# One triangular-solve right-hand side computed as two accumulated products instead of one over stacked operands

## The chip, the cores and the metric

The kernel runs on one core of a Trainium2 chip. The time is the device time of one execution in microseconds (us); three executions are given before the change. The engines are named as in the profile: PE does matrix products, PEld is PE's weight load, DVE, ACT and POOL do element-wise work, SP issues transfers. Each engine works through its own queue of instructions in order and waits at an instruction for its semaphores.

## The reference, cut to what matters

The program is one layer of an encoder with three token mixers that run beside each other: an mLSTM, a long convolution, and a bidirectional RWKV-7 time mixing. The change touches the third alone. With 1024 positions, 16 heads of width 64 and two directions it computes for each head

```python
def step(state, inp):
    r_t, w_t, k_t, v_t, kk_t, a_t = inp
    sa = jnp.einsum('bhij,bhj->bhi', state, -kk_t)
    state = (state * w_t[:, :, None, :] + sa[..., None] * (kk_t * a_t)[:, :, None, :]
             + v_t[..., None] * k_t[:, :, None, :])
    return state, jnp.einsum('bhij,bhj->bhi', state, r_t)
```

once forwards and once backwards, and the outputs of the two directions are added. Everything is float32.

## The kernel before, in words

The projections of the input (`gemm`, L343 to L357) are long rows of matmuls of 128x512: each float32 operand is split into a high and a low part, and three products are summed, hence the lines L351, L352 and L353. Their weights come in by `load_w` (L327): a transfer `wraw`, a rounding to `wh` on ACT (L333), the remainder `wl` on POOL (L334). These projections are jobs in a list, and `fill` advances them by two 128-row pieces at a time.

The RWKV recurrence is computed in chunks of 64 positions. Two heads form a pair that fills 128 partitions (one head in 0 to 63, one in 64 to 127), and both directions go side by side, so eight pairs have 16 chunk steps each: 128 steps in all, in `scan` (L1733). `prep` makes the scaled vectors: `ar` holds alpha (`ar[:, 0]`, from the key directions) and the scaled receptance (`ar[:, 1]`), `bk` holds beta and the scaled keys. `tphase` makes the inverse triangular matrix `tt` of each chunk by a forward substitution on DVE (the many `tm` and `Tb` operations at L476). `setup` (L1659) makes for two chunks at a time the masked Gram matrices `G`, the transposes `B`, and the values in the lower half (partitions 64 to 127) of `SV`.

One step of `scan` is a chain:

- U: a right-hand side, in a bank of PSUM called `pch`. It has a values' part (masked Gram matrix times values) and a state's part (alpha times the state). Before the change both are one product over 128 rows: `G[0:64]` holds a copy of alpha, `SV[0:64]` a copy of the state. In the profile this is `pch<-SV,G`, four matmuls for two heads and two directions.
- `us` is U copied out of PSUM on DVE (L1762). `tt` times `us` gives SA (`pch<-us,tt`).
- SA is copied into `SV[0:64]`, over the state, one head by DVE (L1768), one by ACT (L1769).
- B times `SV` gives the change of the state (`pch<-SV,B`); two DVE operations at L476 add the old state and scale it, giving `sn`, the new state.
- `sn` is copied into the `SV[0:64]` of the next step, one head by DVE (L1793), one by ACT (L1794), and the next U starts.

The outputs of a step are put off into the next one (`late`): a product of `SV` and `G` (`pch<-G,SV`) stands right behind the next U, and a product of state and receptance (`pch<-ar,sn`) right behind the next SA.

What a matmul of float32 costs: the profile shows two records for each of these 64-wide matmuls, so a group of four appears as eight.

The order of an engine's queue is set when the program is built, by the framework's scheduler: it goes by its own estimate of when operands are ready, by priorities (`in_turn` gives the chain's matmuls the highest and keeps each group together in its given order), and by the order in which the code is written. `weave` spreads the projections' jobs evenly over the steps of the scan, so that each pair of chain products has projection matmuls between them on PE.

Of the kernel before, what the change touches and what calls it, by code (L numbers as in the profile page):

```python
# [285 lines left out]
class Trunk:  # L286
# [1060 lines left out]
    def rwkv(self, yc_out, pairs=range(8)):  # L1347
        nc, tc, A = self.nc, self.tc, self.A
        with ExitStack() as c2:
            e = c2.enter_context  # L1350
            cp = e(tc.tile_pool(name="rc", bufs=1))
            self.rp = e(tc.tile_pool(name="rp", bufs=1))
            self.oka = cp.tile([128, 8], F32, name="oka")
            nc.vector.tensor_scalar(self.oka, self.col("ka", 0, 8), -0.5, 1.0, op0=MUL, op1=ADD)


            self.hka = cp.tile([128, 8], F32, name="hka")
            nc.vector.tensor_scalar(self.hka, self.col("ka", 0, 8), 0.5, None, op0=MUL)
            self.hrk = cp.tile([128, 8], F32, name="hrk")
            nc.vector.tensor_scalar(self.hrk, self.col("rk", 0, 8), 0.25, None, op0=MUL)  # L1360
            self.nkk = cp.tile([128, 8], F32, name="nkk")
            nc.vector.tensor_scalar(self.nkk, self.col("kk", 0, 8), -0.5, None, op0=MUL)
            self.hwa = cp.tile([128, 32], F32, name="hwa")
            nc.vector.tensor_scalar(self.hwa, self.col("w0", 0, 32), 0.5, None, op0=MUL)
            self.hlgb = cp.tile([128, 16], F32, name="hlgb")
            nc.vector.tensor_scalar(self.hlgb, self.col("lg", 0, 16), 0.5, None, op0=MUL)
            self.gmask = cp.tile([128, 2, 128], F32, name="gmask")
            nc.sync.dma_start(self.gmask, A["gmask"])
            self.smask = cp.tile([128, 8 * 65], F32, name="smask")
            nc.vector.memset(self.smask, 1.0)  # L1370
            nc.vector.memset(self.smask.rearrange("p (c t) -> p c t", t=65)[:, :, 0:1], 0.0)
            self.bln = cp.tile([128, 1], F32, name="bln")
            nc.vector.memset(self.bln, 10.0 * math.log(2.0))


            self.tt_t = [p.tile([128, 16, CL], F32, name=f"tt{g}", tag=f"tt{g}", bufs=1)
                         for g, p in enumerate((self.ep, cp))]
            self.vp = self.ep.tile([128, T], F32, name="vp", tag="vp", bufs=1)

            self.cmat = cp.tile([128, 128], F32, name="cmat")  # L1380
            self.stt(self.cmat, self.ones_bd, -1.0 / 64.0, self.ident)
            for t in self.tt_t:
                nc.vector.memset(t, 0.0)


            pairs = list(pairs)
            n = len(pairs)
            cx = [dict(p=p, ar={}, al={}, bk={}, pc={}) for p in pairs]
            run(self.load(cx[0]))
            for g in range(2):  # L1390
                for d in range(2):
                    run(self.prep(cx[0], g, d))
                    self.fill(6)
                if g == 0:
                    for _ in self.tphase(cx[0], 0):
                        self.fill(1)
            prep1 = iter(())
            run(self.setup(cx[0], 0))
            for i in range(n):
                at = {}  # L1400

                def put(gen, *steps):
                    for s in steps:
                        at.setdefault(s, []).append(gen)
                put(prep1, 0, 0, 1, 2, 3, 4, 4)
                put(self.bonus(cx[i]), 5, 6, 7)
                put(ahead(tc, self.tphase(cx[i], 1), TP), *range(6, 28, 2))
                if i + 1 < n:
                    nx = cx[i + 1]
                    put(self.load(nx, cx[i - 1] if i else None), 8, 9, 10, 11)  # L1410
                    put(ahead(tc, self.prep(nx, 0, 0), PP), 15, 16, 19, 33, 33)
                    put(ahead(tc, self.prep(nx, 0, 1), PP), 34, 35, 36, 37, 37)
                    put(ahead(tc, self.tphase(nx, 0), TP), *range(39, 62, 2))
                    prep1 = ahead(tc, chain(self.prep(nx, 1, 0), self.prep(nx, 1, 1)), PP)
                    put(prep1, 40, 42, 49)
                if i > 0:
                    put(self.post(cx[i - 1], yc_out, i + 1 == n), 5, 6, 7, 8, 11, 12, 13, 14)
                weave(self.scan(cx[i], cx[i + 1] if i + 1 < n else None), at, self.fill, max(0, self.left() - 6) / (64.0 * (n - i + 0.1)))
            run(self.post(cx[n - 1]))
            return cx[n - 1]["out"]  # L1420
# [106 lines left out]
    def prep(self, cx, g, d):  # L1527

        nc, rp = self.nc, self.rp
        p, r, k, kk, w2, mm = (cx[n] for n in ("p", "r", "k", "kk", "w2", "mm"))  # L1530
# [43 lines left out]
        for q in range(2):  # L1574
            ar = self.ep.tile([128, 4, 2, CL], F32, name="ar", tag="ar", bufs=8)
            bk = self.ep.tile([128, 4, 2, CL], F32, name="bk", tag="bk", bufs=8)
            cs = slice(4 * q, 4 * q + 4)
            self.stt(ar[:, :, 0, :], c8(rd(kk))[:, cs], -2.0, P[:, cs, 0:64], MUL, MUL)
            self.tt(ar[:, :, 1, :], c8(rd(r))[:, cs], P[:, cs, 1:65])
            self.tt(bk[:, :, 0, :], c8(tmp)[:, cs], s[:, cs, 1:65])  # L1580

            self.tt(bk[:, :, 1, :] if d == 0 else bk[:, :, 1, ::-1], c8(a)[:, cs], s[:, cs, 1:65])
            for j in range(2):
                cx["al"][g, d, 2 * q + j] = ar[:, 2 * j:2 * j + 2, 0, :]
            for j in range(4):
                cx["ar"][g, d, 4 * q + j] = ar[:, j]
                cx["bk"][g, d, 4 * q + j] = bk[:, j]
            yield
# [70 lines left out]
    def setup(self, cx, b):  # L1659

        nc, rp, vp = self.nc, self.rp, self.vp
# [3 lines left out]
        g, c = b // 4, 2 * (b % 4)  # L1665
        hsl = (slice(0, 64), slice(64, 128))
        ops = [(j, d, cx["bk"][g, d, c + j], cx["ar"][g, d, c + j]) for j in range(2) for d in range(2)]

        G = rp.tile([128, 2, 2, 2, 128], F32, name="G", tag="G", bufs=2)
# [3 lines left out]
                     for j, d, bk, ar in ops for h in (1, 0))  # L1673
        for h in range(2):
            self.tt(G[:, :, :, h, :], pg[h], self.gmask.unsqueeze(1).broadcast_to([128, 2, 2, 128]))
            for d in range(2):
                nc.scalar.copy(G[0:64, :, d, h, 0:64], cx["al"][g, d, b % 4][hsl[h]])  # L1677
        yield


# [7 lines left out]
        if b < 4:  # L1688

            SV = rp.tile([128, 2, 4, 64], F32, name="SV", tag="SV", bufs=4)  # L1690
            if b == 0:
                nc.gpsimd.memset(SV[0:64], 0.0)
            cx["sv"].append(SV)
            pv = pv[:, 0:256].rearrange("p (e c) -> p e c", e=2)
            for e in range(2):
                t0 = 128 * (7 - b if e else b)
                nc.tensor.matmul(pv[:, e], vp[:, t0:t0 + 128], self.cmat, start=True, stop=True)
            for k in range(2):
                nc.scalar.copy(SV[64:128, :, 2 * k:2 * k + 2].rearrange("p h e x -> p e h x"),
                               pv[hsl[k]].rearrange("p e (h x) -> p e h x", h=2))  # L1700
            at = ((0, 3), (2, 1))
            SV = cx["sv"][b]
        else:
            SV = cx["sv"][7 - b]
            at = ((1, 2), (3, 0))
# [27 lines left out]
    def scan(self, cx, nx):  # L1733

        nc, rp = self.nc, self.rp
        S0 = None
        y = rp.tile([128, T], F32, name="y", tag="y", bufs=1)
        hsl = (slice(0, 64), slice(64, 128))
# [7 lines left out]
        now, late = chunk(0), None  # L1746
        for m in range(16):
            g, c, j = m // 8, m % 8, m % 2
            tt = self.tt_t[g]
            ar = [cx["ar"][g, d, c] for d in range(2)]  # L1750
            G, B, SV, at, both = now
            if j == 0:
                ahead = self.setup(cx, m // 2 + 1) if m < 14 else self.setup(nx, 0) if nx else iter(())
            ch = self.ps.tile([128, 4, 2, CL], F32, name="pch", tag="c", bufs=2)
            U, SA, SN, py = (ch[:, i] for i in range(4))

            ins = self.in_turn(partial(nc.tensor.matmul, U[hsl[h], d], G[:, j, d, h, 0:64], SV[:, h, at[d]],
                                       start=True, stop=True) for d in range(2) for h in (1, 0))
            if late:
                late[0](ins)  # L1760
            us = self.sm.tile([128, 2, CL], F32, name="us", tag="us", bufs=2)
            nc.vector.tensor_copy(us, U)  # L1762
            ins = self.in_turn(partial(nc.tensor.matmul, SA[hsl[h], d], tt[hsl[h], 8 * d + c, :], us[hsl[h], d],
                                       start=True, stop=True) for d in range(2) for h in range(2))
# [18 lines left out]
            S0 = S1  # L1783
# [3 lines left out]
            if m in (7, 15):  # L1787
                late[1](late[0](None))
                late = None
            if m < 15:  # L1790

                SV, at = now[2], now[4]
                nc.vector.tensor_copy(SV[0:64, 0, at], S1[0:64])  # L1793
                nc.scalar.copy(SV[0:64, 1, at], S1[64:128])  # L1794
            yield
            next(ahead, None)
            yield
# [111 lines left out]
```

## Time and profile before

| | us |
|---|---|
| median of three executions | 2141.99 |
| lowest and highest | 2134.19, 2142.42 |
| the profiled execution: its time | 2147.95 |
| the profiled execution: its span, first to last instruction | 2145.5 |
| stretch of the 128 chunk steps, first U to last output, from the span's start | 916 to 1933 |
| mean granted TensorE clock | 0.975 of full speed |

A row of the grouped view reads: line, engine, operation, written tile `<-` read tiles, shapes, `x` how many, then the time in which at least one of them ran, the mean duration of one in ns, and after the second bar the idle time of the engine just before them with what ended it. A row of the timeline reads: start, duration, engine, line, operation. Matmul records overlap, so the distance between two starts tells what one costs PE, not the duration of one.

### The profile page before, as it was taken

To read this page: it belongs to the slowest core of one execution; us is meant where nothing else is said; L and a number is where in the kernel's file an instruction comes from. 1 tells how busy PE (TensorE), PEld (TensorE's weight loads), DVE (VectorE), ACT (ScalarE), POOL (GpSimd) and SP (SyncE) were. 2 spreads that over 40 slices of the span, in tenths; PEclk is the share of its full clock that TensorE was granted. 3 is DMA by queue.
4 is the path that set the end of the run, shared out by engine and by line. 5 is a ranking of instruction groups with operands and counts; after the bars stand their busy time and mean duration, and the time that the engine had idled before them with its cause. 6 is when DMAs were issued, how large, how long until landed. Compare 5 with 4: busy or idle time off the path is not lost.

```text
span 2145.5 us, 45845 instructions
## 1 busy us (share of the span) xinstructions
PE 1981.4 (92%) x17098; PEld 1483.3 (69%) x17098; DVE 1608.9 (75%) x4706; ACT 1078.0 (50%) x2509; POOL 417.1 (19%) x485
## 2 busy tenths in 40 slices
PE   6899899999989989999999999999999979999998
PEld 4666677777868767767666666666666656677776
DVE  4854989988646956878888887877888788855536
ACT  5557357445242214565665656567466764432221
POOL 2211311113232341311111110101111252111200
PEclk9999999999999989999999999999999979999999
DMA  9211222333374425322322323233232443546623
GB/s 260 73 67 62 79 75 82 110 110 108 127 242 169 142 89 184 127 74 73 124 93 98 119 71 134 70 107 124 79 120 80 141 157 122 194 133 231 226 81 131
DMA packets 169383, 262.18 MB, mean 122 GB/s; under 512 B 17863, under 2 KB 87335, under 8 KB 169160
## 3 DMA queue, kind: packets, MB, share of 16 engines
q1 hardware_dynamic: 169160, 259.25, 37.1%
q8 instruction: 134, 2.20, 0.4%
q14 instruction: 89, 0.73, 0.1%
HBM read 181.06 MB, written 78.12 MB: 121 GB/s over the span
## 4 chain that ended last, share of the span: by engine, by line
PE 52%; DVE 20%; ACT 10%; issue 9%; DMA 7%; POOL 2%; SPq 1%; DVEq 0%; ACTq 0%; POOLq 0%
PE pg L351 10%; PE pg L352 10%; PE pg L353 9%; PE pout L1259 4%; PE pch L398 3%; PE pch L395 3%; DVE tm L476 2%; DVE Tb L476 2%; POOL wl L334 2%; PE pG L953 1%; DVE st L473 1%; DVE dw L476 1%; PE pwx L398 1%; PE ptv L1686 1%; PE phs L1426 1%
## 5 line engine op out<-in xcount | busy, mean ns | idle before, releaser
L334 POOL TENSOR_TENSOR wl<-wraw,wh 128x256 fp32r<-128x256 f32 x408 | 366.2, 902 | 1393.9 <-ACT wh L333 1339.2
L351 PE MATMUL pg<-hh,wh 128*128 128x512 f32 x1440 | 602.2, 418 | 20.0 <-ACT wh L333 12.3
L352 PE MATMUL pg<-hh,wl 128*128 128x512 f32 x1440 | 597.1, 415 | 20.1 <-POOL wl L334 20.1
L353 PE MATMUL pg<-hl,wh 128*128 128x512 f32 x1440 | 593.3, 412 | 2.7 <-DVE hl L565 2.6
L351 PEld LDWEIGHTS pg<-hh,wh 128*128 128x128 f32 x1440 | 276.2, 192 | 91.6 <-ACT wh L333 16.5
L352 PEld LDWEIGHTS pg<-hh,wl 128*128 128x128 f32 x1440 | 276.1, 192 | 84.4 <-POOL wl L334 28.0
L353 PEld LDWEIGHTS pg<-hl,wh 128*128 128x128 f32 x1440 | 276.0, 192 | 65.8 <-issue 4.5
L333 ACT CAST wh<-wraw 128x256 fp32r<-128x256 f32 x408 | 162.0, 404 | 210.0 <-PE pg L353 133.5
L476 DVE TENSOR_TENSOR tm<-Ab,Tb 128x126 f32<-128x126 f32 (+22 forms) x496 | 142.3, 287 | 5.9 <-DMA Tb<-in_tinit 1.5
L476 DVE TENSOR_TENSOR Tb<-Tb,tm 128x126 f32<-128x126 f32 (+22 forms) x496 | 140.2, 283 | 4.3
L1677 ACT COPY G<-ar 64x128 f32<-64x128 f32 x256 | 64.2, 295 | 74.8 <-DVE G L476 72.5
L457 ACT ACTIVATE st<-pg 128x512 f32<-128x512 f32 x74 | 44.2, 598 | 112.1 <-PE pg L353 108.4
L473 DVE SCALAR_TENSOR_TENSOR st<-pg,hmu,st 128x511 f32<-128x511 f32 (+1 forms) x130 | 80.9, 635 | 24.7 <-ACT e L424 17.4
L476 DVE TENSOR_TENSOR G<-pgr,gmask 128x512 f32<-128x512 f32 x128 | 85.6, 680 | 8.5 <-PE pgr L398 7.9
L473 DVE SCALAR_TENSOR_TENSOR st<-st,pg 128x512 f32<-128x512 f32 x80 | 54.3, 680 | 31.3 <-PE pg L353 10.0
L476 DVE TENSOR_TENSOR sn<-pch,sn 128x128 f32<-128x128 f32 x120 | 34.4, 286 | 55.6 <-PE pch L398 42.7
L141 DVE SCALAR_TENSOR_TENSOR row<-row 64x1 f32<-64x1 f32 x393 | 73.5, 211 | 2.1
L398 PE MATMUL pgr<-ar,bk 64*128 64x128 f32 x896 | 74.9, 282 | 0.0
L1769 ACT COPY SV<-pch 64x128 f32<-64x128 f32 x128 | 33.6, 263 | 69.7 <-DVE SV L1768 67.1
L476 DVE TENSOR_TENSOR dw<-dw,dw 128x512 f32<-128x512 f32 x92 | 66.5, 753 | 0.9
L417 ACT ACTIVATE st<-pg,omu 128x512 f32<-128x512 f32 x52 | 35.7, 689 | 58.0 <-PE pg L353 54.7
L1762 DVE COPY us<-pch 128x128 f32<-128x128 f32 x128 | 36.5, 285 | 36.5 <-PE pch L398 35.7
(674 smaller groups left out, 4117.4 us busy)
## 6 DMA issues: line engine op xcount, KB each, us to landing
wraw<-in_w_in SPq DMA_DIRECT2D x340, 128.0 KB, 2.3
low<-lora SPq DMA_DIRECT2D x32, 512.0 KB, 3.9
sig<-st SPq DMA_DIRECT2D x48, 256.0 KB, 2.6
st<-sig SPq DMA_DIRECT2D x48, 256.0 KB, 3.3
wraw<-in_w_br SPq DMA_DIRECT2D x68, 128.0 KB, 2.9
adw<-in_ada_w SPq DMA_DIRECT2D x16, 512.0 KB, 7.4
x<-in_x SPq DMA_DIRECT2D x8, 512.0 KB, 6.4
hx<-st SPq DMA_DIRECT2D x16, 256.0 KB, 2.0
```

The costliest lines, as they stand in the source:

```text
L141: self.ops.append(lambda: self.nc.vector.scalar_tensor_tensor(o, a, s, b, op0=op0, op1=op1))
L333: self.nc.scalar.copy(hi, raw)
L334: self.nc.gpsimd.tensor_tensor(lo, raw, hi.bitcast(F32), op=SUB)
L351: nc.tensor.matmul(p, wh, hh, start=(k == 0), stop=False)
L352: nc.tensor.matmul(p, wl, hh, start=False, stop=False)
L353: nc.tensor.matmul(p, wh, hl, start=False, stop=(k == n - 1))
L395: ins = f()
L398: ins = f()
L473: return self.nc.vector.scalar_tensor_tensor(out, in0, s, in1, op0=op0, op1=op1)
L476: return self.nc.vector.tensor_tensor(out, a, b, op=op)
L1259: nc.tensor.matmul(p, a_[:, ts], w[:, b_], start=(n == 0), stop=(n == 23))
L1677: nc.scalar.copy(G[0:64, :, d, h, 0:64], cx["al"][g, d, b % 4][hsl[h]])
```

## The change

U becomes two accumulated products in the same bank. The first is `G` times `SV` as before, over 128 rows, but `G[0:64]` keeps the zeros that its mask leaves there, so only the values count; it reads nothing of the running step's state. The second is alpha, read in place from `ar`, times the state, read in place from `sn`, over 64 rows for each head; it is left out in the first step of a pair, where the state is zero. The copies of alpha into `G` (in `setup`) and of the state into `SV` (in `scan`) go. `SV[0:64]` is cleared on POOL for all four `SV` tiles of a pair instead of the first, since it must hold finite numbers when it meets the zeros.

```diff
@@ setup
             self.tt(G[:, :, :, h, :], pg[h], self.gmask.unsqueeze(1).broadcast_to([128, 2, 2, 128]))
-            for d in range(2):
-                nc.scalar.copy(G[0:64, :, d, h, 0:64], cx["al"][g, d, b % 4][hsl[h]])
...
             SV = rp.tile([128, 2, 4, 64], F32, name="SV", tag="SV", bufs=4)
-            if b == 0:
-                nc.gpsimd.memset(SV[0:64], 0.0)
+            nc.gpsimd.memset(SV[0:64], 0.0)
@@ scan
             ins = self.in_turn(partial(nc.tensor.matmul, U[hsl[h], d], G[:, j, d, h, 0:64], SV[:, h, at[d]],
-                                       start=True, stop=True) for d in range(2) for h in (1, 0))
+                                       start=m == 0 or d == 0, stop=m == 0)
+                               for d in range(2) for h in (1, 0))
             if late:
                 late[0](ins)
+            if m:
+                self.in_turn(partial(nc.tensor.matmul, U[hsl[h], d], ar[d][hsl[h], 0, :], S0[hsl[h], d],
+                                     start=False, stop=d == 1) for d in range(2) for h in range(2))
             us = self.sm.tile([128, 2, CL], F32, name="us", tag="us", bufs=2)
...
-            if m < 15:
-
-                SV, at = now[2], now[4]
-                nc.vector.tensor_copy(SV[0:64, 0, at], S1[0:64])
-                nc.scalar.copy(SV[0:64, 1, at], S1[64:128])
```

The scheduler makes a new order of it. The first place is PE's queue in one chunk step of the third pair, from U to SA. Before, `pch<-SV,G` is U, `pch<-G,SV` the put-off output, `pch<-us,tt` SA, `pch<-ar,sn` the other put-off output, and `pg` the projections:

```order
L352 MATMUL pg<-hh_132,wl 128x512
L395 MATMUL pch<-SV,G 64x64
L398 MATMUL pch<-SV,G 64x64 x3
L398 MATMUL pch<-G,SV 64x64 x4
L353 MATMUL pg<-hl_133,wh 128x512
L351 MATMUL pg<-hh_134,wh 128x512
L352 MATMUL pg<-hh_134,wl 128x512
L395 MATMUL pch<-us,tt_8479 64x64
L398 MATMUL pch<-us,tt_8479 64x64 x3
L398 MATMUL pch<-ar,sn 64x64 x4
```

The same step in the changed kernel, where `pch<-sn,ar` is the new state's part of U:

```order
L395 MATMUL pch<-SV,G 64x64
L398 MATMUL pch<-SV,G 64x64 x3
L351 MATMUL pg<-hh_144,wh 128x512
L398 MATMUL pch<-G,SV 64x64 x4
L352 MATMUL pg<-hh_144,wl 128x512
L395 MATMUL pch<-sn,ar 64x64
L398 MATMUL pch<-sn,ar 64x64 x3
L353 MATMUL pg<-hl_145,wh 128x512
L351 MATMUL pg<-hh_146,wh 128x512
L352 MATMUL pg<-hh_146,wl 128x512
L395 MATMUL pch<-us,tt_8479 64x64
L398 MATMUL pch<-us,tt_8479 64x64 x3
```

Where one run of two groups stood between projections, three runs of one group each now stand.

The second place is ACT's queue in the setup of the first chunks, before (-) and now (+); `tt` and `B` are named above, and `kk` belongs to the next pair:

```order
 L1451 ACTIVATE kk<-k,pv 128x1024
-L1656 COPY tt_8478<-pwx 32x16x32 x2
-L333 CAST wh<-wraw 128x256
-L1677 COPY G<-ar 64x2x64 x2
-L333 CAST wh<-wraw 128x256
-L1677 COPY G<-ar 64x2x64 x2
-L1687 COPY B<-ptv 128x512
+L1654 COPY tt_8478<-pwx 32x16x32 x2
+L333 CAST wh<-wraw 128x256 x2
+L1683 COPY B<-ptv 128x512
 L1432 ACT_TABLE_LOAD
```

The four copies of alpha are gone and the two weight roundings stand together; the later lines are the same code with smaller numbers.

The third place is POOL's queue of the changed kernel around the beginning of the second pair, where `wl` are weight remainders, `s` another cleared tile, and `SV` the tiles above:

```order
L1548 MEMSET s 128x8
L1687 MEMSET SV 64x512
L334 TENSOR_TENSOR wl<-wraw,wh 128x256
L1687 MEMSET SV 64x512
L334 TENSOR_TENSOR wl<-wraw,wh 128x256 x3
L1687 MEMSET SV 64x512
L334 TENSOR_TENSOR wl<-wraw,wh 128x256
L1687 MEMSET SV 64x512
```

Before, one clearing of `SV` stood here; now four stand among the weight remainders.

More of the change, by code (lines that the diff above doesn't have):

```diff
@@ L1387, in rwkv @@
             n = len(pairs)
-            cx = [dict(p=p, ar={}, al={}, bk={}, pc={}) for p in pairs]
+            cx = [dict(p=p, ar={}, bk={}, pc={}) for p in pairs]
             run(self.load(cx[0]))
@@ L1582, in prep @@
             self.tt(bk[:, :, 1, :] if d == 0 else bk[:, :, 1, ::-1], c8(a)[:, cs], s[:, cs, 1:65])
-            for j in range(2):
-                cx["al"][g, d, 2 * q + j] = ar[:, 2 * j:2 * j + 2, 0, :]
             for j in range(4):
```

## The prediction

> **What bounds the kernel now.** I read the page's head first, then its chain of work that ended last, then the busy time of the stretch in which the 128 chunk steps run.
>
> ```profile
> span 2145.5 us, 45845 instructions
> PE 1981.4 (92%) x17098; PEld 1483.3 (69%) x17098; DVE 1608.9 (75%) x4706; ACT 1078.0 (50%) x2509; POOL 417.1 (19%) x485
> PE 52%; DVE 20%; ACT 10%; issue 9%; DMA 7%; POOL 2%; SPq 1%; DVEq 0%; ACTq 0%; POOLq 0%
> 916.00:1933.00 1017.00, 943.64 (x12128) 677.88 (x12129) 823.90 (x2422) 608.77 (x1518) 161.62 (x209) 0.98 0.34 112
> ```
>
> The last row gives, for 916 to 1933 us, the length, then PE, PEld, DVE, ACT and POOL busy, clock, DMA. PE is busy for 943.6 of 1017 us, so 73.4 us are idle. A step takes 1017/128 = 7.95 us, of which PE works 7.4. PE is the bound here, with DVE (81%) behind it. So a change of the scan is to be priced as PE time first, and a shorter chain pays only as far as PE stands idle for it. Where it stands idle is in the groups of the same stretch:
>
> ```profile
> L398 PE MATMUL pch<-SV,G 128*64 128x64 f32 x768 | 58.3, 233 | 3.5 <-DVE SV L1793 3.4
> L398 PE MATMUL pch<-ar,sn 64*64 64x64 f32 x952 | 49.0, 222 | 0.0
> L395 PE MATMUL pch<-SV,B 128*64 128x64 f32 x256 | 42.8, 250 | 12.5 <-ACT SV L1769 11.6
> L395 PE MATMUL pch<-SV,G 128*64 128x64 f32 x256 | 42.1, 246 | 13.1 <-ACT SV L1794 12.6
> L395 PE MATMUL pch<-us,tt 64*64 64x64 f32 x256 | 41.7, 243 | 15.5 <-DVE us L1762 15.1
> ```
>
> Ahead of U (`SV,G`) PE idles 13.1 + 3.5 = 16.6 us in all, nearly all of it for the two copies of the state that the change removes. Ahead of SA (`us,tt`) it idles 15.5, ahead of the state's product (`SV,B`) 12.5.
>
> **The change part by part.** First what is added on PE: a state's part of U in 15 of 16 steps of 8 pairs, 120 groups of four matmuls. Its form, 64 rows by 64 columns in two head halves, is that of `pch<-ar,sn`, which the kernel already runs 120 times. What such a group costs is read from the distances between the starts of neighbouring matmuls; three places of the timeline:
>
> ```profile
> 1381.41 0.40 PE L351 MATMUL pg<-hh,wh 128*128 128x512 f32 x1
> 1381.74 0.27 PE L395 MATMUL pch<-SV,G 128*64 128x64 f32 x1
> ...
> 1382.02 0.40 PE L398 MATMUL pch<-G,SV 128*64 128x64 f32 x8
> 1382.35 0.50 PE L352 MATMUL pg<-hh,wl 128*128 128x512 f32 x1
> 1382.69 0.40 PE L353 MATMUL pg<-hl,wh 128*128 128x512 f32 x1
> ...
> 1383.96 0.39 PE L352 MATMUL pg<-hh,wl 128*128 128x512 f32 x1
> 1384.19 0.39 PE L353 MATMUL pg<-hl,wh 128*128 128x512 f32 x1
> ...
> 1385.11 0.39 PE L351 MATMUL pg<-hh,wh 128*128 128x512 f32 x1
> 1385.43 0.27 PE L395 MATMUL pch<-SV,B 128*64 128x64 f32 x1
> ...
> 1385.81 0.50 PE L352 MATMUL pg<-hh,wl 128*128 128x512 f32 x1
> 1386.15 0.39 PE L353 MATMUL pg<-hl,wh 128*128 128x512 f32 x1
> ...
> 1883.95 0.40 PE L353 MATMUL pg<-hl,wh 128*128 128x512 f32 x1
> 1884.27 0.27 PE L395 MATMUL pch<-G,SV 128*64 128x64 f32 x1
> ...
> 1884.65 0.45 PE L398 MATMUL pch<-ar,sn 64*64 64x64 f32 x8
> 1885.03 0.50 PE L351 MATMUL pg<-hh,wh 128*128 128x512 f32 x1
> 1885.38 0.39 PE L352 MATMUL pg<-hh,wl 128*128 128x512 f32 x1
> ```
>
> Projections alone follow each other every 0.23 us (1383.96 to 1384.19). From a projection's start to the second start after a run of groups there are two such slots, 0.46, and the rest is the run. One group: 1385.11 to 1386.15 is 1.04, so 0.58. Two groups of the same shape (`SV,G` and `G,SV`): 1381.41 to 1382.69 is 1.28, so 0.82. The second group thus costs 0.24, and the way in and out of a run costs 0.58 - 0.24 = 0.34, waits aside. Two groups of different shape (`G,SV` over 128 rows, `ar,sn` over 64): 1883.95 to 1885.38 is 1.43, so 0.97: the change of shape inside the run costs 0.15.
>
> A rule of the Trainium skill, "TensorEngine Tiling (Array Packing)", section "Key Properties", speaks against the change here: changing the tiling mode, not just the tile, drains the engine, and 128x64 and 64x64 are two modes. The trace agrees, with the 0.15 us between 0.82 and 0.97; by the row of equal shapes alone the sum below would be 10 us less.
>
> Next, how often. Counted over PE's whole order, the groups stand in 409 runs before and in 495 after, and a change between 128 and 64 rows falls inside a run 17 times before and 83 after. Hence: 120 groups x 0.24 = 29 us; 86 more runs x 0.34 = 29 us; 66 more changes x 0.15 = 10 us; together 68 us. Bounds: 29 us if ways in and out all fall into time in which PE would have waited; 120 x 0.58 + 10 = 80 us if every added group stood alone. I take 68, since it is what the order says.
>
> Now what the chain gains. One step, from the new state to the next U:
>
> ```profile
> 1386.40 0.29 DVE L476 TENSOR_TENSOR sn<-sn,pc 128x128 f32<-128x128 f32 x1
> ...
> 1386.79 0.21 DVE L1793 COPY SV<-sn 64x128 f32<-64x128 f32 x1
> ...
> 1387.29 0.30 ACT L1794 COPY SV<-sn 64x128 f32<-64x128 f32 x1
> ...
> 1387.64 0.27 PE L395 MATMUL pch<-SV,G 128*64 128x64 f32 x1
> ```
>
> The state is ready at 1386.69, the second copy ends at 1387.59, U starts 0.05 later. The removed piece is 0.90 us here; the copies' own 0.30 is its least. It buys PE time only out of the 16.6 us above. Not all of them: the scheduler also moves the state's product nearer (by the order's median, 5 projection matmuls stand between `SV,B` and U's state part, 6 before between `SV,B` and U), and what stays ahead of it, `sn` on a busy DVE, is then late. I take 10 us, with 0 and 16.6 as bounds.
>
> The engines beside PE lose work:
>
> ```profile
> L1677 ACT COPY G<-ar 64x128 f32<-64x128 f32 x252 | 63.2, 295 | 73.2 <-DVE G L476 70.9
> L1793 DVE COPY SV<-sn 64x128 f32<-64x128 f32 x120 | 29.3, 244 | 1.4 <-PE pch L398 0.4
> L1794 ACT COPY SV<-sn 64x128 f32<-64x128 f32 x120 | 35.6, 296 | 45.8 <-DVE sn L476 41.3 <-PE pch L398 2.5
> ```
>
> ACT loses 63.2 + 35.6 = 98.8 of its 608.8 us, a sixth, and 73.2 us of standing at the head of its queue for `G`'s mask on DVE; behind those copies stand the copies of SA that `SV,B` waits for. DVE loses 29.3 of 823.9. ACT and DVE are covered by PE's work, so this is worth nothing by itself; it shortens the waits ahead of SA and the state's product, 15.5 + 12.5 = 28 us. A quarter of them, 7 us, is my choice (bounds 0 and 28). Where the last chain runs over DVE (20% of it) its 29.3 us count: 6 us. For the weights that PE waits for I add 4 us, with 0 and 9.2 as bounds:
>
> ```profile
> PE plw L1545 <- DMA low<-lora: 5.4, 5, 2.1
> PE pg L352 <- POOL wl L334: 4.7, 5, 1.2
> PE pgr L395 <- ACT q L1615: 3.6, 5, 1.2
> L1692 POOL MEMSET SV<- x8: 517/519/528, 742.8 to 1785.9; 64x512 f32 x8
> ```
>
> These are waits of PE in the same stretch (total us, times, longest); `wl` 4.7 and `q` 3.6 hang on ACT, `low` on transfers that nothing here alters. The removed waits come to 10 + 7 + 6 + 4 = 27 us.
>
> The last row is the price of POOL's clearing, 0.52 us each. 24 more are 12.5 us on an engine that is 16% busy in the stretch, and each is issued in the setup of its two chunks, a step or more (7.95 us) ahead of them; I price them at 0. Without that cover a values' product would wait for a clearing behind a `wl`, up to the 1.2 us of the longest `wl` wait: 24 x 1.2 = 29 us.
>
> The wait that the change adds is that of U's state part on `sn`. Behind it on PE stand, in order, the projections and SA. The values' part does not wait for the state: it runs where U did not start before, and costs there what it costs.
>
> The sum: 68 - 27 = +41 us, from the profiled execution's 2147.95 to 2189; that execution lies 6 us above the median, so 2141.99 + 41 = 2183 for the median.
>
> **The rivals.** *The transition is no occupancy (faster).* The 0.34 at the ends of a run may be a latency that is paid only where PE goes from waiting to working; then the values' part, which waits for nothing, costs 0.24 in the stream and so does the state's part: 29 us added. All three waits of the chain (16.6 + 28 = 44.6) go, with the shorter chain and the lighter ACT. 29 - 45 = -16: 2126. For it: over half of the idle time in front of chain products is put down to copies. Against: the 0.58 of a single group stands where its transition has a projection before and after, and PE's idle time of 73.4 would have to shrink by 45 while the work grows. It decides from 40 us of waits saved. Chance 0.11.
>
> *It cancels (the same).* The products fall partly into idle time: 45 us of cost against 40 of gain, for which the same rows speak: +5, 2147. Chance 0.14.
>
> *Nothing is saved (slower still).* The state's product is placed so near that PE waits for `sn` as it did for the copies, and runs are broken more than the order of one step tells: 80 us and no gain, or 68 with half of POOL's 29 on top: +81, 2223. For it: the median distance falls from 6 to 5. Against: the copies' least 0.30 is longer than the one projection, 0.23. Chance 0.13.
>
> *The chain sets the step.* If 7.95 us were the chain and projections mere filling, 120 x 0.90 = 108 us would go: 2034. PE's 93% speak against it, and 943.6 + 68 = 1012 of 1017 us leave no room. Chance 0.02.
>
> **How the numbers follow.** The forecast of 2183 has a chance of 0.60; its own range, from costs of 60 to 80 and gains of 12 to 45, is 2157 to 2210. For 8 in 10 I go to 2134 below, which takes in cancelling, and 2218 above, short of the middle of the third rival. What a measurement can tell from no change is about 0.5%, 10.7 us. Slower by more than that: 0.60 + 0.13 = 0.73; within it 0.14; faster 0.11 + 0.02 = 0.13.
>
> **What would show it.** In the groups of the changed kernel: 960 records of `pch<-sn,ar` at about 49 to 95 us busy, PE's busy time in the scan near 1010 us and the scan near 1058 us; the idle time ahead of `sn,ar` under 10 us and owed to `sn` on DVE; no `G<-ar` and no `SV<-sn`; ACT near 510 us in the stretch; a run of `G,SV` and `sn,ar` between projections at 0.97 us. The forecast is wrong if the scan is no longer than 1030 us: then single groups cost PE less than 0.58, or over 45 us of waits went. It is wrong upwards if PE waits for `sn` as long as it did for the copies, or for a clearing of `SV`.

## The result

The changed kernel takes 2169.17 us (median of 4, 2167.03 to 2179.75) against 2139.68 us before (4 runs, 2134.19 to 2142.42): a ratio of 1.0151, 95% interval 1.0110 to 1.0192. It is slower, by 29.5 us; the forecast was +41 us, 2183 in a range of 2134 to 2218.

The profiled execution of the changed kernel took 2167.43 us. The page's head, and the stretch from the first `us` copy to the last output (length, then PE, PEld, DVE, ACT and POOL busy, clock, DMA):

```profile
span 2165.7 us, 47221 instructions
PE 2027.9 (94%) x18058; PEld 1512.5 (70%) x18058; DVE 1593.8 (74%) x4586; ACT 984.4 (45%) x2137; POOL 426.2 (20%) x509
908.00:1955.00 1047.00, 995.06 (x13086) 710.41 (x13083) 807.57 (x2302) 515.63 (x1147) 174.06 (x230) 0.99 0.33 108
```

The same stretch of the kernel before is 917 to 1934 us:

```profile
917.00:1934.00 1017.00, 943.64 (x12134) 678.15 (x12133) 824.82 (x2424) 608.24 (x1517) 162.21 (x210) 0.98 0.34 112
```

The scan takes 30 us more, 1047 against 1017. It begins 9 us earlier (908 against 917), so the profiled spans differ by less, 20.2 us. Of the 9 us ahead, the clock accounts for about 7 (by the traces' clock records 22 us are lost to it there, 29 before); the rest is not explained. PE has 960 more matmul records in the whole kernel and is busy 51 us longer in the scan; DVE and ACT are relieved of 17 and 93 us; PE's idle time falls from 73.4 to 51.9 us. Where it is left, by groups in the changed kernel's scan:

```profile
L398 PE MATMUL pch<-G,SV 128*64 128x64 f32 x992 | 56.3, 230 | 6.9 <-DVE sn L476 6.3 <-issue 0.5
L398 PE MATMUL pch<-sn,ar 64*64 64x64 f32 x720 | 53.0, 227 | 0.0
L395 PE MATMUL pch<-us,tt 64*64 64x64 f32 x256 | 41.7, 243 | 7.3 <-DVE us L1762 6.9
L395 PE MATMUL pch<-SV,B 128*64 128x64 f32 x256 | 41.4, 244 | 16.6 <-ACT SV L1769 16.0
L395 PE MATMUL pch<-SV,G 128*64 128x64 f32 x256 | 41.0, 242 | 0.8 <-DVE y L476 0.7
L395 PE MATMUL pch<-sn,ar 64*64 64x64 f32 x240 | 38.9, 242 | 7.1 <-DVE sn L476 6.8
```

The values' part (`SV,G`) no longer waits: 0.8 us. But PE still waits for the new state, `sn`: 7.1 us ahead of the state's part and 6.3 ahead of the put-off output product (`G,SV`), together 13.4 where the copies had cost 16.6 before. The output product reads nothing of `sn`; it writes a quarter of the bank from which `sn` is made. Before the change it mostly stood behind a U that had waited for the copies; now the values' part ahead of it waits for nothing. It waits for `sn` in experiment 2 as well, where no state's part is left, so the wait is its own. Ahead of SA the idle time is halved (15.5 to 7.3); ahead of the state's product it has grown (12.5 to 16.6). The new groups cost what such groups cost before. Three groups in one run, with a change from 128 to 64 rows after the second:

```profile
1136.52 0.40 PE L353 MATMUL pg<-hl,wh 128*128 128x512 f32 x1
1136.85 0.27 PE L395 MATMUL pch<-SV,G 128*64 128x64 f32 x1
...
1137.13 0.40 PE L398 MATMUL pch<-G,SV 128*64 128x64 f32 x8
1137.46 0.27 PE L395 MATMUL pch<-sn,ar 64*64 64x64 f32 x1
...
1137.84 0.50 PE L351 MATMUL pg<-hh,wh 128*128 128x512 f32 x1
1138.18 0.39 PE L352 MATMUL pg<-hh,wl 128*128 128x512 f32 x1
```

From 1136.52 to 1138.18 are 1.66 us, less two projections' 0.46: 1.20, against 0.34 + 3 x 0.24 + 0.15 = 1.21 by the prices of the prediction.

### The profile page after: what moved, and what is told of

It reads as the page before. It is cut to its first block, busy times and chain, and to the rows that moved or that the text cites. A ratio compares the mean times of both kernels' runs of the same rounds, so it can differ in the third digit from the quotient of the medians.

```text
span 2165.7 us, 47221 instructions
## 1 busy us (share of the span) xinstructions
PE 2027.9 (94%) x18058; PEld 1512.5 (70%) x18058; DVE 1593.8 (74%) x4586; ACT 984.4 (45%) x2137; POOL 426.2 (20%) x509
## 4 chain that ended last, share of the span: by engine, by line
PE 31%; DVE 11%; issue 7%; ACT 5%; DMA 3%; POOL 1%; SPq 0%; DVEq 0%; POOLq 0%; ACTq 0%
PE pg L351 4%; PE pg L353 4%; PE pg L352 4%; PE pout L1259 4%; PE pch L398 4%; PE pch L395 4%; DVE tm L476 1%; DVE Tb L476 1%; PE phs L1426 1%; PE ptv L1682 1%; PE pwx L398 1%; DVE s L1557 1%; PE pgr L398 1%; POOL wl L334 1%; DVE bk L476 1%
## 5 line engine op out<-in xcount | busy, mean ns | idle before, releaser
L352 PE MATMUL pg<-hh,wl 128*128 128x512 f32 x1440 | 592.2, 411 | 15.6 <-POOL wl L334 15.5
L398 PEld LDWEIGHTS pgr<-ar,bk 64*128 64x128 f32 x896 | 63.7, 190 | 0.7
```

What stands on the lines that cost most here:

```text
L352: nc.tensor.matmul(p, wl, hh, start=False, stop=False)
L398: ins = f()
```

## An account that the experiments are to close

Three things are put together for each kernel, against the kernel before. The price: groups x 0.24, runs x 0.34, changes of shape inside a run x 0.15, counted over PE's order. The change of PE's idle time in the scan. And the TensorE clock, which I had not counted: its mean over the profiled span differs from kernel to kernel. The numbers of runs and changes stand in the expectations; experiment 3 has 405 runs and 20 changes. Of before, of the change, and of experiments 1 to 5 in their order:

```profile
core 0: 2145.5 us, clock 0.975
```

```profile
core 0: 2165.7 us, clock 0.986
```

```profile
core 0: 2171.5 us, clock 0.983
```

```profile
core 0: 2143.0 us, clock 0.976
```

```profile
core 0: 2150.6 us, clock 0.974
```

```profile
core 0: 2151.8 us, clock 0.981
```

```profile
core 0: 2185.2 us, clock 0.984
```

As an estimate, one hundredth of clock over a span of 2145 us is taken as 21 us. The last columns are the difference of the profiled spans and of the medians of the timed runs.

| kernel | price | idle | clock | sum | span | median |
|---|---|---|---|---|---|---|
| the change | +68 | -21 | -24 | +23 | +20 | +30 |
| 1 extra group | +47 | 0 | -17 | +30 | +26 | +41 |
| 2 no state's product | +10 | -10 | -2 | -2 | -3 | +11 |
| 3 no copies of alpha | -1 | +2 | +2 | +3 | +5 | +13 |
| 4 joined | +24 | -6 | -13 | +5 | +6 | +15 |
| 5 doubled | +92 | -26 | -19 | +47 | +40 | +51 |

The sums meet the spans within 7 us for all six. The medians' differences lie 8 to 15 us above the spans', since the profiled execution of the kernel before (2147.95) lies 8 us above the median of its timed runs.

The idle time is measured, so what the table tests is price and clock as an account of PE's busy time. That can be done for the scan alone. By the clock records of the traces, the time lost there to the lower clock is 20.5 us before and 6.8, 13.7, 23.9, 22.2, 13.7 and 8.5 us in the six kernels. The price and the change of that loss give +54, +40, +14, +1, +17 and +80 us of PE's busy time; measured are +51, +38, +16, +2, +18 and +76.

## Experiment 1: the added product alone

```diff
 # the kernel before
+            if m:
+                self.in_turn(partial(nc.tensor.matmul, SN[hsl[h], d], ar[d][hsl[h], 0, :], S0[hsl[h], d],
+                                     start=True, stop=True) for d in range(2) for h in range(2))
             us = self.sm.tile([128, 2, CL], F32, name="us", tag="us", bufs=2)
```

> The kernel before, with the state's product added and thrown away: in 15 of 16 steps the four 64x64 matmuls of alpha and state are also run, into the quarter of the bank that the state's product overwrites later. Nothing is removed. By PE's order this is 120 more groups, 7 more runs (409 to 416) and 104 more changes of shape inside a run (17 to 121). Theory (PE time as priced: 0.24 a group, 0.34 a run, 0.15 a change): 29 + 2 + 16 = 47 us more than before, 2175 to 2195. Rival (the added matmuls fall into time in which PE idles, and the change is slow because of its order and its waits): 0 to 15 us more, 2140 to 2155.

Measured: 2179.61 us (6 runs) against 2138.97 (24), ratio 1.0199 (1.0166 to 1.0232), +41 us. The theory's range holds it, the rival's does not. The scan:

```profile
907.00:1962.00 1055.00, 981.38 (x13083) 711.64 (x13080) 825.47 (x2422) 604.77 (x1514) 162.78 (x209) 0.99 0.32 108
```

PE idles 1055 - 981.4 = 73.6 us, as much as before the change (73.4): 120 more groups did not fall into the time in which PE waits. They are PE time.

## Experiment 2: the change without the added product

```diff
 # the changed kernel
-                                       start=m == 0 or d == 0, stop=m == 0)
+                                       start=True, stop=True)
...
-            if m:
-                self.in_turn(partial(nc.tensor.matmul, U[hsl[h], d], ar[d][hsl[h], 0, :], S0[hsl[h], d],
-                                     start=False, stop=d == 1) for d in range(2) for h in range(2))
```

> The changed kernel without the state's product (U lacks the state's part, so the recurrence is another): no group of sn and ar, and U waits for no state. PE's order has 423 runs instead of 495 and 53 changes of shape instead of 83. Theory: 29 + 24 + 5 = 58 us of products, and the 14 us that PE idles for the state, less than the changed kernel: 2095 to 2115. Rival (products fall into idle time; the slowdown is POOL's clearing and the order, which stay): 10 to 25 us less, 2145 to 2160.

Measured: 2149.52 us (12 runs), ratio to before 1.0043 (1.0016 to 1.0070), 20 us less than the changed kernel. The theory's range fails: I had taken 58 us of products and 14 us of waits off the changed kernel. The rival's range holds the time, but two of its reasons fall: products in idle time with experiment 1, POOL's clearing with experiment 9. The order is left. What happened is in the scan, and in the group of the put-off output:

```profile
908.00:1931.00 1023.00, 959.46 (x12126) 684.70 (x12124) 800.32 (x2301) 510.02 (x1143) 174.12 (x230) 0.98 0.33 111
```

```profile
L398 PE MATMUL pch<-G,SV 128*64 128x64 f32 x992 | 56.8, 232 | 8.9 <-DVE sn L476 8.9
```

With as many matmuls as before, no product in U that reads the state, and ACT relieved of 98 us, PE still idles 63.5 us. All copies together thus give 10 us of PE's idle time, and the order that the scheduler makes of it (423 runs instead of 409, 53 changes instead of 17: 10 us by price) takes them back. And taking the product out of the changed kernel gives back only 20 to 23 us of its 58, since 11.6 us of idle time return and the clock falls from 0.986 to 0.976, 21 us over the span. My expectation subtracted a price without adding what fills the gap.

## Experiment 3: the copies of alpha alone

```diff
 # the kernel before
-            for d in range(2):
-                nc.scalar.copy(G[0:64, :, d, h, 0:64], cx["al"][g, d, b % 4][hsl[h]])
```

> The kernel before without the copies of alpha (G keeps its zeros, so U lacks the state's part and the recurrence is another); the copies of the state, the products and the chain stay. ACT loses 63 us of work and its waits for G's mask. Theory (ACT is covered by PE): 3 to 10 us less than before, 2130 to 2137. Rival (ACT's queue holds the chain up, since 28 us of PE's idle time hang on SA and its copies): 15 to 30 us less, 2110 to 2125.

Measured: 2152.13 us (12 runs), ratio 1.0040 (1.0016 to 1.0064). Neither range holds it: 58 us less work on ACT make nothing faster, and by 0.4% slower. The scan and its groups show why nothing is gained:

```profile
917.00:1938.00 1021.00, 945.95 (x12143) 683.74 (x12144) 818.02 (x2424) 550.40 (x1266) 162.64 (x211) 0.98 0.34 112
```

```profile
L395 PE MATMUL pch<-SV,B 128*64 128x64 f32 x256 | 42.6, 249 | 20.5 <-ACT SV L1767 19.8
L395 PE MATMUL pch<-SV,G 128*64 128x64 f32 x256 | 42.5, 248 | 10.9 <-ACT SV L1792 10.1
L395 PE MATMUL pch<-us,tt 64*64 64x64 f32 x256 | 42.0, 245 | 13.1 <-DVE us L1760 12.7
```

Ahead of U and SA PE waits 2 us less each than before (13.1 and 15.5), ahead of the state's product 8 us more (12.5). The wait moves along the chain: the scheduler makes a new order, and in it the chip is late at another of the chain's products. The 7 us that I had put down to the lighter ACT are not there. Why it is slower, by 9 us by the ratio and 13 by the medians, is not settled; price, idle time and clock explain 3.

## Experiment 4: fewer runs with the same groups

The values' product of the next step and the put-off output are issued right behind the state's product, three groups of equal shape in one run.

```diff
 # the changed kernel
+        def values(m, now, ins):
+            G, B, SV, at, both = now
+            ch = self.ps.tile([128, 4, 2, CL], F32, name="pch", tag="c", bufs=2)
+            U = ch[:, 0]
+            self.in_turn((partial(nc.tensor.matmul, U[hsl[h], d], G[:, m % 2, d, h, 0:64], SV[:, h, at[d]],
...
-            self.in_turn(partial(nc.tensor.matmul, SN[hsl[h], d], B[:, j, d, hsl[h]], SV[:, h, at[d]],
+            ins = self.in_turn(partial(nc.tensor.matmul, SN[hsl[h], d], B[:, j, d, hsl[h]], SV[:, h, at[d]],
...
+            own, late = self.outputs(y, py, m, S0, ar, now)
+            ins = own(ins)
+            if m < 15:
+                now = chunk(m + 1)
+                ch1 = values(m + 1, now, ins)
```

> The changed kernel with its values' product and its put-off output moved behind the state's product of the step before, as one run of three groups of equal shape: the same groups, but 402 runs instead of 495 and 1 change of shape inside a run instead of 83. Theory: 93 x 0.34 + 82 x 0.15 = 44 us less than the changed kernel, less whatever the longer run makes wait: 2122 to 2145. Rival (ways in and out of a run are waits and no occupancy): the changed kernel's time within 12 us, 2157 to 2180.

Measured: 2153.75 us (6 runs), ratio to before 1.0082 (1.0050 to 1.0114), 15 us less than the changed kernel. The direction is the theory's, the size is not: 44 us were priced. The scan, and two of its groups:

```profile
907.00:1936.00 1029.00, 961.66 (x13090) 696.42 (x13089) 806.73 (x2301) 514.25 (x1147) 169.23 (x230) 0.99 0.33 110
```

```profile
L395 PE MATMUL pch<-SV,B 128*64 128x64 f32 x256 | 42.2, 247 | 22.1 <-ACT SV L1775 21.4
L395 PE MATMUL pch<-sn,ar 64*64 64x64 f32 x240 | 39.2, 244 | 18.5 <-DVE sn L476 18.5
```

PE is busy 33.4 us less than in the changed kernel with the same groups, and about 40 less when the clock's loss in the scan (6.8 against 13.7) is set aside: that is near the 44 priced. But its idle time is 67.3 us, 15 more: a third of what is saved on runs and changes, PE spends waiting, above all for `sn` (18.5 instead of 13.4) and for the copies of SA (22.1 instead of 16.6).

## Experiment 5: the added product twice

```diff
 # the changed kernel
-                self.in_turn(partial(nc.tensor.matmul, U[hsl[h], d], ar[d][hsl[h], 0, :], S0[hsl[h], d],
-                                     start=False, stop=d == 1) for d in range(2) for h in range(2))
+                ins = self.in_turn(partial(nc.tensor.matmul, U[hsl[h], d], ar[d][hsl[h], 0, :], S0[hsl[h], d],
+                                           start=False, stop=d == 1) for d in range(2) for h in range(2))
+                self.in_turn((partial(nc.tensor.matmul, SN[hsl[h], d], ar[d][hsl[h], 0, :], S0[hsl[h], d],
+                                      start=True, stop=True) for d in range(2) for h in range(2)), ins)
```

> The changed kernel with the state's product run twice in the same run of matmuls, the second time into the quarter of the bank that the state's product of the step overwrites later. 120 more groups of equal shape, 482 runs instead of 495, 81 changes of shape instead of 83. Theory (a group costs 0.24 us wherever it stands): 29 - 4 = 24 us more than the changed kernel, 2184 to 2200. Rival (what costs is the run's ends and the wait, the matmuls themselves overlap with what follows): 4 us less to 8 us more, 2164 to 2177.

Measured: 2192.59 us (6 runs) against 2141.74 (17), ratio 1.0249 (1.0216 to 1.0282), 23 us more than the changed kernel's 2169.17; expected were 24. The scan:

```profile
907.00:1974.00 1067.00, 1019.66 (x14047) 738.05 (x14048) 805.45 (x2303) 515.07 (x1148) 171.14 (x230) 0.99 0.32 106
```

PE is busy 24.6 us longer than in the changed kernel. A group in a run costs about 0.24 us on PE also behind another of its kind; the rival falls.

## Experiments 6 and 7: SV cleared once, with four tiles

```diff
# the changed kernel (6) and the joined one (7)
+            self.svt = [self.rp.tile([128, 2, 4, 64], F32, name=f"SV{x}", tag=f"SV{x}", bufs=1) for x in range(4)]
+            for x in self.svt:
+                nc.gpsimd.memset(x[0:64], 0.0)
...
-            SV = rp.tile([128, 2, 4, 64], F32, name="SV", tag="SV", bufs=4)
-            nc.gpsimd.memset(SV[0:64], 0.0)
+            SV = self.svt[b]
```

> The changed kernel with four fixed SV tiles that are cleared once for all eight pairs instead of in each: 28 clearings on POOL fewer, and with them POOL's waits for PE to be done with a tile (70.6 us in 16 waits in the changed kernel). PE's order has 485 runs instead of 495 and 92 changes instead of 83. Theory (POOL's clearing is covered, priced at 0): within 6 us of the changed kernel, 2160 to 2175. Rival (clearings hold up the weights' remainders behind them): 10 to 25 us less, 2144 to 2159.

> The joined order (state's product, put-off output and next values' product as one run) with SV cleared once: 395 runs instead of 402, 9 changes of shape instead of 1. Theory: no different from the joined kernel's 2153.75 within 6 us, 2148 to 2160, so still slower than before, since the 120 added groups stay. Rival (POOL's clearing counts): 2130 to 2145, level with the kernel before.

Measured: 2196.82 us (6 runs; ratio to before 1.0250, 1.0215 to 1.0285) and, joined, 2160.35 us (5 runs; 1.0084, 1.0055 to 1.0113). Neither answers its question: the setup of the next pair writes its values into the first tile while the last step of a pair has still to read it, so that step works on wrong values, and PE's order is another. Their times say nothing about POOL. Experiments 9 and 10 put the question again with five tiles, for the changed kernel and for the joined one.

## Experiment 8: the kernel before with its output product moved

```diff
 # the kernel before: own() behind the state's product of its step instead of behind the next U
-            if late:
-                late[0](ins)
...
+            own, late = self.outputs(y, py, m, S0, ar, now)
+            own(ins)
```

> The kernel before with the put-off output product (SV and G) moved from behind U to behind the state's product of its own step; nothing else. 406 runs instead of 409 and 3 changes of shape instead of 17, the same groups: by price 1 + 2 = 3 us less. Theory: 2130 to 2140, 0 to 9 us less than before, not to be told from it. Rival (the put-off output keeps SA waiting and PE idle after U): 10 to 20 us less, 2119 to 2129.

Measured: 2142.31 us (12 runs) against 2141.74, ratio 1.0006 (0.9982 to 1.0029). No difference, as the theory had it, though 2 us above its range: an order of PE with as many groups and runs takes as long.

## Experiments 9 and 10: SV cleared once, with five tiles

POOL's clearing had been priced at nothing, and the changed kernel's waits gave reason to doubt it (total us, times, longest):

```profile
POOL SV L1687 <- PE pch L398: 70.6, 16, 14.4
```

```diff
# five tiles are made and cleared at the beginning, as above four
...
-            SV = rp.tile([128, 2, 4, 64], F32, name="SV", tag="SV", bufs=4)
-            nc.gpsimd.memset(SV[0:64], 0.0)
+            SV = self.svt[self.svn % 5]
+            self.svn += 1
```

> The changed kernel with five fixed SV tiles in turn, cleared once at the beginning, in place of four buffers cleared for each pair: 27 clearings fewer on POOL, none of them waiting for PE, and PE's order row by row that of the changed kernel (495 runs, 83 changes of shape). Theory (POOL's clearing is covered): within 6 us of the changed kernel, 2163 to 2175. Rival (the 70.6 us that clearings wait for PE hold up the weights' remainders): 10 to 25 us less, 2144 to 2159.

> The joined order with five fixed SV tiles cleared once; PE's order is that of the joined kernel (402 runs, 1 change). Theory: the joined kernel's 2153.75 within 6 us, so 0.4 to 1% above the kernel before. Rival: 2130 to 2145, level with the kernel before.

Measured: 2168.44 us (6 runs; ratio to before 1.0147, 1.0105 to 1.0188) against the changed kernel's 2169.17; and joined 2157.50 us (12 runs; 1.0078, 1.0050 to 1.0105) against 2153.75. The clearing costs nothing that can be told from no change, POOL's waits with it. That the weight remainders behind them are needed later would explain it; no run shows this by itself. No kernel of these beats the one before; the best form of the two products, joined, is still 0.8% behind it.

## Why the prediction was right

*The bound.* PE was named as the bound, and PE's account closes. Experiment 1 shows it for added work (47 us by price, 41 measured, PE's idle time unchanged), experiment 3 from the other side: ACT's relief is worth nothing.

*The price of the added products*, 68 us, stands: 0.24 for a group was met by doubling it (24 expected, 23 measured), and 1.20 us for a run of three by the timeline. In the scan PE's busy time rose by 51 us, and by 65 when the 14 us that the clock gave back there are set aside. The change of shape is in that 1.20 as well. The 0.34 for a run's ends is not shown apart from it: in experiment 4 both went together, about 40 of 44 us, and a third of the 44 came back as waits.

*The gains*, 27 us, are the terms that were mis-sized, and that the idle time fell by 21 us all the same is luck: no part of it has the size it was given. Ahead of U I had 10 us; it was 16.6 - 13.4 - 0.8 = 2.4, because the state's part and the put-off output wait for `sn` on DVE instead. The prediction had named `sn` as what is late next, but not the output. For ACT and DVE relieved I had 7 us ahead of SA and the state's product; it was 8 saved at the one and 4 lost at the other. The 6 us for DVE's part of the last chain are seen in no run. For the weights that PE waits for I had 4 us, with a bound of 9.2, though the two rows that it named, `wl` 4.7 and `q` 3.6, make 8.3. It was 13.3 of 13.7: `q` is gone, `low` (5.4) too, which I had taken as untouched, and this is left:

```profile
PE pg L352 <- POOL wl L334: 0.4, 1, 0.4
```

The lighter ACT is not the whole reason for that: the same three waits are 5.9 us with all copies gone (experiment 2) and 5.7 with the product added and nothing removed (experiment 1). The 21 us do not split into causes either. 10 came with the copies (experiment 2) and 11.6 when the product was added to that kernel; but the product added to the kernel before left the idle time as it was (experiment 1).

*What was left out* is the clock: 0.986 instead of 0.975 in the profiled runs, 24 us over the span. About half of that is a matter of which executions were profiled: the middle of the clocks of the changed kernel's four runs is 0.9835, the median of 24 runs of the kernel before 0.978, which makes 12 us, and 68 - 21 - 12 = 35 beside the 29.5 measured. In the scan alone the profiled runs differ by 14 us: the stretches of lower clock in the kernel before and, second, in the changed one are (length first, clock third from the end)

```profile
1192.00:1196.00 4.00, 3.96 (x30) 2.84 (x31) 2.36 (x10) 1.33 (x5) 0.00 (x0) 0.57 0.66 214
...
1492.00:1510.00 18.00, 16.63 (x246) 12.21 (x245) 13.32 (x44) 7.87 (x23) 0.11 (x1) 0.81 0.14 51
...
1714.00:1725.00 11.00, 7.92 (x24) 5.40 (x25) 10.90 (x17) 4.79 (x13) 8.68 (x8) 0.53 0.55 185
...
1735.00:1752.00 17.00, 11.65 (x179) 9.06 (x178) 9.38 (x23) 13.33 (x27) 3.94 (x5) 0.50 0.42 130
...
1779.00:1783.00 4.00, 3.51 (x29) 2.46 (x29) 3.18 (x14) 0.67 (x2) 0.60 (x1) 0.57 0.00 0
```

```profile
1044.00:1049.00 5.00, 5.00 (x30) 2.89 (x30) 3.73 (x12) 0.00 (x0) 0.00 (x0) 0.66 0.12 31
...
1198.00:1202.00 4.00, 3.83 (x16) 3.08 (x17) 3.84 (x12) 1.24 (x2) 0.00 (x0) 0.57 0.48 159
...
1737.00:1741.00 4.00, 4.00 (x33) 2.89 (x30) 3.66 (x12) 0.93 (x3) 0.00 (x0) 0.60 0.92 302
...
1792.00:1796.00 4.00, 4.00 (x28) 2.93 (x28) 3.87 (x12) 2.53 (x6) 1.08 (x1) 0.57 0.40 150
```

Length times lost share comes to 20.5 us before and 6.7 after. So the scan's +30 us are 68 - 21 - 14 = 33. The page's row of clock digits had shown the dips before the change; I took them as the same after it.

*The signs that were named.* PE's busy time in the scan is 995 us (near 1010 expected) and the scan 1047 (near 1058); both are short by about the clock's 14 us. ACT is busy 516 us there (near 510). Ahead of `sn,ar` PE idles 7.1 us, owed to `sn` (under 10). With the output's share it is 13.4, not far from the 16.6 of the copies, which would have meant an error upwards.

*The rivals.* That the way in and out is no occupancy, and so the change faster, fell with the result, and with experiment 4: fewer runs and changes with the same groups took 33 us off PE's busy time. Experiments 1 and 5 show the groups themselves as PE time. That cost and gain cancel fell too, since 29.5 us is far outside the 10.7 that was set for no change; and so did the chain as the bound, which would have made the kernel faster. "Nothing is saved" came nearest in one point: PE waits for `sn` nearly as it did for the copies.

## What to carry to other kernels

Where one engine is busy for over nine tenths of a stretch, price a change there in that engine's time first, by the distance between starts in its timeline, and count runs and changes of shape over the whole order, not at one place. A wait taken out of a chain that a scheduler weaves into other work is not yet time saved: in the change and in experiments 3 and 4 much of it turned up at another link. And a sum of such a stretch needs a line for the clock, which differed by 0.011 between the two profiled runs, 24 us here.

## What the runs showed of the hardware that I had not expected

The granted clock differs between kernels, and between runs of one kernel, by as much as the terms of the sum. Over 24 timed runs of the kernel before its mean lies between 0.973 and 0.985 and the time between 2152 and 2130 us; the medians of the clock are 0.978 for the kernel before, 0.9815 with 120 more groups and 0.983 with the product doubled. More work on PE went with a higher clock there. But how well PE is filled does not settle it: experiment 1 idles as long in the scan as the kernel before, and experiment 6 idles less, 59.9 us, at a lower clock (0.97 in this row, a median of 0.976 in its timed runs):

```profile
917.00:1988.00 1071.00, 1011.15 (x13092) 722.83 (x13092) 805.22 (x2303) 510.49 (x1143) 157.00 (x202) 0.97 0.32 106
```

Whether the clock falls because PE idles, or both have another cause, no run here separates. In the kernel before it was at 0.50 from 1735 to 1752 us though PE's longest waits around that place were about 2 us:

```profile
PE pg L352 <- POOL wl L334: 2.7, 3, 1.2
PE plw L1545 <- DMA low<-lora: 2.1, 1, 2.1
PE pch L395 <- ACT SV L1769: 2.0, 1, 2.0
```

These are the largest entries of PE's waits from 1705 to 1755 us (total, times, longest); `plw` is a product that reads the transferred `low`. In the changed kernel the dip at 1737 us stands behind a longer wait:

```profile
1736.80 0.27 PE L395 MATMUL pch<-sn,ar 64*64 64x64 f32 x1 [4.05 <-DVE sn L476]
```

The Trainium skill, "TensorE: Matmul & The Clock Gate", section "HAM oscillation — how this bites in real kernels", has the rule that PE gaps above some 3.4 us bring the clock down. The 4.05 us agree with it; the place of the kernel before shows that several short gaps near each other go with a lower clock as well.
